# Moving the operand splits in front of the attention units to other buffers, other engines and a later place

## The chip, the cores and the metric

The kernel runs on one core of one Trainium2 chip. A core has a matrix engine (TensorE, PE in the profile), three engines for elementwise work (VectorE or DVE, ScalarE or ACT, GpSimd or POOL), and queues that start DMAs (SP's, ACT's and POOL's). The metric is the device time of one execution in microseconds (us), lower is better. The kernel before was timed three times: 1029.26, 1029.71 and 1030.7 us, median 1029.71 us. One further execution was profiled.

## The reference: what is computed

One layer of a transformer-like block on 1024 latent tokens (a 16 by 64 grid) and 256 context tokens of width 1024. The part around the change is the two-dimensional neighbourhood attention: each token attends to an 8 by 16 window of the grid, with a learned relative position bias, and to all context tokens in the same softmax.

```python
u_x, q_x, k_x, v_x = _project(h_x, w_in[l])
u_c, q_c, k_c, v_c = _project(h_c, w_in[l])
...
s_loc = jnp.einsum('bnqhd,brnkhd->bhnqrk', q_r, k_b).astype(jnp.float32) * scale
s_loc = jnp.where(col_mask, s_loc + bias.astype(jnp.float32), -jnp.inf)
s_ctx = jnp.einsum('bnqhd,bkhd->bhnqk', q_r, k_ctx).astype(jnp.float32) * scale
s = jnp.concatenate([s_loc.reshape(B, H, NA_NCB, NA_QB, n_loc), s_ctx], axis=-1)
p = jax.nn.softmax(s, axis=-1).astype(v.dtype)
...
o = (jnp.einsum('bhnqrk,brnkhd->bnqhd', p_loc, v_b) + jnp.einsum('bhnqk,bkhd->bnqhd', p_ctx, v_ctx))
...
mix_x = jnp.concatenate([_pool_mixer(u_x, pool_w[l], pool_scale[l]), attn_x], axis=-1) @ w_out[l]
x = x + gt1 * _rmsnorm(mix_x, g_post_mix[l])
y_x = _sq_relu_mlp(_modulate(x, g_pre_mlp[l], sh2, sc2), w_mlp_in[l], w_mlp_out[l])
x = x + gt2 * _rmsnorm(y_x, g_post_mlp[l])
```

All numbers are float32.

## The kernel before, in words

**Products in parts.** To keep float32 accuracy, an operand of a product is split into a high part (rounded to the matrix engine's fp32r type) and a low part (what is left), and a product is three matmuls: high by high, high by low, low by high (function three, L197 to L200). A split is one copy for the high part and one subtraction for the low part: split (L156) makes the copy on ACT (L146) and the subtraction on DVE (L152).

**Keys and queries.** The eight heads are worked in four pairs j = 0 to 3. Keys and queries come from a seven-product scheme (Strassen's kind) with products called P1 to P7. Each product is made for K and for Q and for j = 0 and 1, and is twelve matmuls (half_product, L950); kept_product (L931) adds its bank into the tiles kT[j] and q. The list of steps in front of the attention, L959, ends with step 20 and 21 (P7 of K, j = 0 and 1) and step 22 and 23 (P4 of K, "the last key product"). P7 and P4 of Q (last_query, L1195) stand behind that loop. In the profile the K products write the banks pK, the last Q products the banks pqv.

**Parts of keys and queries.** key_parts(j, b) (L904) splits half b (columns 512 b to 512 b + 511) of kT[j] into kP{j}h and kP{j}l, and query_parts(j, b) (L910) splits q of pair j, half b, into qP{j}_{b}. Both go through apart (L894): with pool set, both instructions are POOL's (L896 and L897), otherwise ACT's and DVE's. Their buffers come from one of two sets: with spare set from the "hl" set of eight tiles (whl), which the weights of the seven products use as well, two for each; otherwise from the "pg" set of 33 tiles (page), which holds nearly everything else: tokens' parts (hx, S3h), kT, q, the bias tables, values and so on.

**Units.** The attention is 32 units i = 8 j + m: pair j, block m of 128 tokens. Around the first units the program's order is: scores(i) (PE, banks S; then two DVE instructions, L1033, one for each head e, which add the bias table and find the least value), the jobs of unit i (L1211), turn(i - 2) (18 or 22 transposes on PE, L1064, of which the first take shares[i - 2], a POOL copy rb, L1050), exps(i, 0), the kept turns (L1083, one on ACT and one on DVE), exps(i, 1) (ACT, L1044), last_query("P4", i) for i = 0 and 1, and values(i - 3) (PE, L1098). share(i - 1) is called inside scores(i), behind its first L1033: a reciprocal on DVE and the copy rb on POOL. The banks S of a unit are two, for e = 0 and 1, and there are two in all, so scores(i + 1) need the L1033 of unit i.

**The order.** A list scheduler places instructions and grants buffers; a set of in_order blocks fixes the program's order of each engine inside a block. The loop of steps is one block (pooling, L956), and what follows is another (projected, L1193), with POOL in a block of its own (first_pool, L1190). Between the two blocks the order on an engine is the scheduler's. On POOL, the program's order around the first units is: the tables' memsets (L872), two accumulating DMAs add_to(s3, s1a) at i = 1 and two at i = 2 (issued at L188, y<-y in the profile), rb at scores(i), and three table instructions (L885) for each call of built.

Of the kernel before, what the change touches and what calls it, by code (L numbers as in the profile page):

```python
# [11 lines left out]
F32 = mybir.dt.float32  # L12
# [68 lines left out]
def hybrid_block(ctx, tc, x, ctx_in, w_mod, b_mod, gp1, gp2, w_in, pool_w, rpb, w_out, w1, w2, vectors,  # L81
                 mask, edge, out):
    nc = tc.nc
    sub, mul, add = ALU.subtract, ALU.mult, ALU.add
# [59 lines left out]
    def high_part(src, hi, factor=1.0):  # L144
        if factor == 1.0:
            nc.scalar.copy(hi, src)  # L146
        else:
            nc.scalar.activation(hi, src, AF.Copy, scale=factor)
# [7 lines left out]
    def split(src, hi, lo, factor=1.0):  # L156
        high_part(src, hi, factor)
        low_part(src, hi, lo, factor)
# [112 lines left out]
    with tc.tile_pool(name="ps1", bufs=6, space=PSUM) as ps1, tc.tile_pool(name="tmp1", bufs=3) as tmp:  # L271
# [276 lines left out]
        for k in range(2):  # L548
            hi, lo = hx[0][k][:, :512], hx[0][k][:, 512:]
# [342 lines left out]
        kparts, qparts, kcs = [None] * 4, {}, []  # L892

        def apart(src, hi, lo, pool):  # L894
            if pool:
                nc.gpsimd.tensor_copy(hi, src)  # L896
                nc.gpsimd.tensor_tensor(lo, src, hi.bitcast(F32), sub)  # L897
            else:
                split(src, hi, lo)

        def part_page(name, spare):
            return whl.tile([P, 1024], F32R, tag="hl", name=name) if spare else page(name, F32R)

        def key_parts(j, b, spare=False, pool=False):  # L904
            if kparts[j] is None:
                kparts[j] = [part_page(f"kP{j}{n}", spare) for n in "hl"]
            bs = slice(b * 512, b * 512 + 512)
            apart(kT[j][:, bs], kparts[j][0][:, bs], kparts[j][1][:, bs], pool)

        def query_parts(j, b, spare=False, pool=False):  # L910
            t = part_page(f"qP{j}_{b}", spare)
            qparts[j, b] = t[:, :512], t[:, 512:]
            apart(qT[j][b], *qparts[j, b], pool)
# [42 lines left out]
        with in_order(ET.PE, ET.Pool, ET.Activation, ET.DVE, ET.SP) as pooling:  # L956
            banks = {of: [bank(f"p{of}{j}") for j in range(2)] for of in "KQ"}
            use(-1)
            for step, (n, of, j) in enumerate([(n, of, j) for n, of in products for j in range(2)]):  # L959
                half_product(n, of, j, banks[of])  # L960
                use(step)
                if step in (5, 9, 17):
                    name = {5: "S1", 9: "S4", 17: "S3"}[step]
                    parts = token_operand(name, sraw[name])
                if step in (5, 7, 9, 11, 17, 19):
                    next(parts)
                    next(parts)
                if step in (7, 11):
                    name = {7: "S4", 11: "S3"}[step]
                    sraw[name] = token_raw(name)  # L970
                if step == 14:
                    mask_page()
                if step == 20:
                    for _ in tables(0):
                        pass
                if step in (21, 22):
                    for g in range(2):
                        pool_mixed(2 * (step - 21) + g)
                kept_product(n, of, j, banks[of][j])
                if step == 10:  # L980
                    kcs += [page(f"kc{n}", F32R) for n in "hl"]
                    split(kcp, *kcs)
                if step == 20:
                    key_parts(0, 0)
                if step == 22:
                    query_parts(0, 0, True)


    with (
# [50 lines left out]
        def exps(i, e):  # L1040
            if e == 0:
                sums[i] = sm(f"su_{i}", 2, 4)
            sp = probs[i, e]
            nc.scalar.activation(sp, sp, AF.Exp, bias=least[i, e], scale=-1.0, accum_out=sums[i][:, e : e + 1])  # L1044
# [148 lines left out]
        with in_order(ET.PE, ET.Activation, ET.DVE, ET.SP) as projected:  # L1193

            def last_query(n, j):  # L1195
                half_product(n, "Q", j, last_queries)
                kept_product(n, "Q", j, last_queries[j])

            key_parts(0, 1)
            key_parts(1, 0, True)  # L1200
            query_parts(1, 0, True)
            last_query("P7", 0)
            key_parts(1, 1)
            last_query("P7", 1)
            key_parts(2, 0, True)
            query_parts(2, 0)

            table = [None] + [tables(j) for j in (1, 2, 3)]
            built = lambda j: next(table[j])
            out_of = lambda n: mod_out(n, accs[n])  # L1210
            jobs = {0: [(built, 1), (key_parts, 2, 1)], 1: [(built, 1)], 2: [(built, 1)], 3: [(built, 1)], 4: [(built, 1)],  # L1211
                    5: [(out_of, "a")], 6: [(out_of, "sc")], 7: [(query_parts, 1, 1, True, True)],
                    8: [(mixed_split, 0, True)], 9: [(built, 2), (out_of, "sh")],
                    10: [(columns_of, "sc", scale2), (built, 2)], 12: [(columns_of, "sh", s2), (built, 2)],
                    13: [(built, 2), (built, 2)], 14: [(query_parts, 3, 0, False, True)],
# [5 lines left out]
            for i in range(N + 4):  # L1221
                if i in LOADS:
                    weight_load(0, kks[LOADS.index(i)])
                if i == N:
                    t1 = [out_load(f"to1_{kk}w", kk, 1) for kk in (0, 1)]
                    b22 = [out_load(f"bo22_{kk}w", kk, 1) for kk in (2, 3)]
                    t3 = [out_load(f"to3_{kk}w", kk, 1) for kk in (2, 3)]
                    for to, kk in zip(t1, (0, 1)):
                        add_to(halved(to), out_block(kk, 0))
                if i == N - 2:  # L1230
                    G1 = gate_page("a")
                if i > 3:
                    weighed(i - 4)
                    if i % 8 == 3:
                        j = i // 8 - 1
                        add_to(s1a[j], heads[j][:, 512:])
                        add_to(sa2[j], heads[j][:, 512:])

                rest_of_bank = lambda name: pz[:, 256:]
                if i == 0:  # L1240
                    gain = mod_gain(gp1, att.tile([P, 256], F32, tag="gp", name="gpa"), nc.sync)
                if i == 4:
                    mod_gate("a", accs["a"], gain, rest_of_bank)
                    accs["sh"] = page("accsh2")
                    nc.sync.dma_start(accs["sh"], kept_row)
                if i == 5:
                    column_sums("sc", accs["sc"], rest_of_bank)
                if i == 8:
                    column_sums("sh", accs["sh"], rest_of_bank)
                if i in (1, 2):  # L1250
                    with tc.issue_after(pooling[ET.Pool]):
                        for k in (2 * i - 2, 2 * i - 1):
                            add_to(s3[k], s1a[k])
                if i in (5, 6):
                    for k in (2 * i - 10, 2 * i - 9):
                        nc.sync.dma_start(sa2[k], s3[k])
                if 8 < i < N and i % 8 == 7:
                    j = i // 8 - 1
                    add_to(heads[j][:, :512], sa2[j])
                low()  # L1260
                if i == N:
                    mixed_split(3)
                for n, at in enumerate(HALVES):
                    if at == i:
                        weight_split(n)
                if i < N:
                    scores(i)
                    for f, *args in jobs.get(i, ()):
                        f(*args)
                else:  # L1270

                    t = i - N
                    if t == 0:
                        x, s1 = [], halves_of("so1_")
                    if t % 2 == 0:
                        xs = ps_s.tile([P, 1024], F32, tag="S", name=f"pox{t}")
                        x += [xs[:, :512], xs[:, 512:]]
                    out_sums(x[t], "A11", wo, t, True)
                    nc.scalar.copy(s1[t], x[t])
                if 1 < i <= N + 1:  # L1280
                    turn(i - 2)
                    fifth_kept(i - 2)
                if i < N:
                    exps(i, 0)
                if 1 < i <= N + 1:
                    turn_kept(i - 2, 0, nc.scalar.copy)
                if i < N:
                    exps(i, 1)
                if 1 < i <= N + 1:
                    turn_kept(i - 2, 1, nc.vector.tensor_copy)  # L1290
                if i < 2:
                    last_query("P4", i)
                if i == N:
                    share(i - 1)
                if 2 < i <= N + 2:
                    values(i - 3)
                if i == 1:
                    query_parts(0, 1)
                if i > N:
                    out_operand("S1", i - N - 1, s1a[i - N - 1])  # L1300
# [752 lines left out]
```

## Time and profile before

| | before |
|---|---|
| median of 3 runs | 1029.71 us |
| profiled execution | 1031.34 us |
| span of its core, first to last instruction | 1029.6 us |
| PE busy | 1014.6 us, 99% of the span |
| DVE busy | 747.1 us |
| ACT busy | 546.8 us |
| POOL busy | 142.6 us |
| mean granted PE clock | 0.996 |
| first scores (unit 0) start | 220.80 us |
| scores of unit 2 start | 231.05 us |

Times within the profile count from the span's start. A row of the timeline gives start, duration, engine, line, operation, output <- inputs, shape and count; in brackets stands how long the engine had been idle before it and which instruction ended that. A row of windows gives, for a stretch, the busy time of each engine with the number of its instructions, the granted PE clock (1.00 is full speed), the share of the DMA engines and the GB/s.

### The profile page before, as it was taken

To read this page: it belongs to the slowest core of one execution; us is meant where nothing else is said; L and a number is where in the kernel's file an instruction comes from. 1 tells how busy PE (TensorE), PEld (TensorE's weight loads), DVE (VectorE), ACT (ScalarE), POOL (GpSimd) and SP (SyncE) were. 2 spreads that over 40 slices of the span, in tenths; PEclk is the share of its full clock that TensorE was granted. 3 is DMA by queue.
4 is the path that set the end of the run, shared out by engine and by line. 5 is a ranking of instruction groups with operands and counts; after the bars stand their busy time and mean duration, and the time that the engine had idled before them with its cause. 6 is when DMAs were issued, how large, how long until landed. Compare 5 with 4: busy or idle time off the path is not lost.

```text
span 1029.6 us, 16022 instructions
## 1 busy us (share of the span) xinstructions
PE 1014.6 (99%) x5910; PEld 840.7 (82%) x5910; DVE 747.1 (73%) x1160; ACT 546.8 (53%) x945; POOL 142.6 (14%) x225
## 2 busy tenths in 40 slices
PE   8999999999999999999999999999999999999997
PEld 7788888878898788888888888888888888888885
DVE  5588757857886687878998888755766666556576
ACT  7573254338897556776655554545543334334431
POOL 3011110126774311410000000000000000000001
PEclk9999999999999999999999999999999999999999
DMA  9999798623338966785776667537967766556556
GB/s 343 333 255 338 248 257 303 204 48 97 74 94 215 214 180 190 262 229 186 260 262 202 216 204 230 189 123 242 337 218 263 254 222 220 201 183 190 172 185 210
DMA packets 123134, 222.70 MB, mean 216 GB/s; under 512 B 9456, under 2 KB 55152, under 8 KB 123056
## 3 DMA queue, kind: packets, MB, share of 16 engines
q1 hardware_dynamic: 96560, 171.14, 50.6%
q0 software_dynamic: 9360, 19.58, 9.4%
q10 hardware_dynamic: 17136, 30.97, 8.1%
q8 instruction: 46, 0.75, 0.3%
q14 instruction: 32, 0.26, 0.1%
HBM read 168.16 MB, written 52.45 MB: 214 GB/s over the span
## 4 chain that ended last, share of the span: by engine, by line
PE 94%; DMA 2%; DVE 1%; issue 0%; ACT 0%; POOL 0%; SPq 0%; DVEq 0%; POOLq 0%; ACTq 0%
PE pu L449 4%; PE pa L1098 4%; PE S L1018 3%; PE phz L198 3%; PE phv L198 3%; PE phx L198 3%; PE pyx L198 3%; PE phx L200 3%; PE pyx L200 3%; PE phz L200 3%; PE pyx L199 3%; PE pyv L198 3%; PE pyz L199 3%; PE pyv L199 3%; PE phv L200 3%; PE pyz L198 3%
## 5 line engine op out<-in xcount | busy, mean ns | idle before, releaser
L1044 ACT ACTIVATE sp<-sp,nm 128x640 f32<-128x640 f32 (+1 forms) x64 | 51.5, 804 | 11.4 <-DVE nm L1033 5.3
L1033 DVE CUSTOM_DVE_ANT_0 sp<-S,tab 128x640 f32<-128x640 f32 (+1 forms) x56 | 44.5, 795 | 14.2 <-PE pz L1064 10.3
L1639 ACT ACTIVATE c<-c 128x512 f32<-128x512 f32 x48 | 30.3, 631 | 44.8 <-DVE c L1759 25.7
L146 ACT CAST wpS<-S 128x512 fp32r<-128x512 f32 x64 | 38.8, 616 | 27.4 <-PE phv L200 9.5
L198 PE MATMUL phx<-thB,wpA 128*128 128x512 f32 x128 | 50.2, 392 | 0.0
L200 PE MATMUL phx<-thB,wpA 128*128 128x512 f32 x128 | 49.8, 389 | 0.0
L199 PE MATMUL phx<-tlB,wpA 128*128 128x512 f32 x128 | 49.8, 389 | 0.0
L152 DVE TENSOR_TENSOR wpS<-S,wpS 128x512 fp32r<-128x512 f32 x64 | 43.4, 685 | 7.4 <-ACT wpS L146 7.4
L140 POOL TENSOR_TENSOR ry<-vy,nhalf 128x1 f32<-128x1 f32 x8 | 5.9, 740 | 281.5 <-DVE vy L138 281.5
L1640 ACT ACTIVATE c<-c 128x512 f32<-128x512 f32 x48 | 30.3, 630 | 15.6 <-DVE sa L1722 12.1
L198 PEld LDWEIGHTS phx<-thB,wpA 128*128 128x128 f32 x128 | 24.0, 188 | 5.4 <-ACT s L1690 0.5
L200 PEld LDWEIGHTS phx<-thB,wpA 128*128 128x128 f32 x128 | 24.0, 188 | 5.1
L199 PEld LDWEIGHTS phx<-tlB,wpA 128*128 128x128 f32 x128 | 24.0, 188 | 4.8
L1098 PE MATMUL pa<-pt,v 128*64 128x128 f32 x352 | 25.9, 280 | 0.2
L1083 DVE COPY pt<-T 128x512 f32<-128x512 f32 x32 | 21.9, 686 | 5.6 <-PE T L1064 5.6
L198 PE MATMUL phz<-thB,wpS 128*128 128x512 f32 x64 | 25.0, 391 | 0.0
L198 PE MATMUL phv<-thT,wpA 128*128 128x512 f32 x64 | 25.0, 391 | 0.0
L199 PE MATMUL phz<-tlB,wpS 128*128 128x512 f32 x64 | 24.9, 390 | 0.0
L199 PE MATMUL phv<-tlT,wpA 128*128 128x512 f32 x64 | 24.9, 389 | 0.0
L200 PE MATMUL phz<-thB,wpS 128*128 128x512 f32 x64 | 24.9, 389 | 0.0
L199 PE MATMUL phy<-tlT,wpS 128*128 128x512 f32 x64 | 24.9, 389 | 0.0
L200 PE MATMUL phy<-thT,wpS 128*128 128x512 f32 x64 | 24.9, 389 | 0.0
(1133 smaller groups left out, 3431.8 us busy)
## 6 DMA issues: line engine op xcount, KB each, us to landing
b<-in_w SPq DMA_DIRECT2D x64, 512.0 KB, 4.6
hrS<-hdS SPq DMA_DIRECT2D x32, 512.0 KB, 5.0
hrA<-hdA SPq DMA_DIRECT2D x24, 512.0 KB, 5.8
wm<-in_w_mod SPq DMA_DIRECT2D x16, 512.0 KB, 9.8
wa_0w<-in_w SPq DMA_DIRECT2D x16, 512.0 KB, 5.0
wa_1w<-in_w SPq DMA_DIRECT2D x16, 512.0 KB, 4.4
hdA<-c ACTq DMA_DIRECT2D x32, 256.0 KB, 2.9
hdS<-sa ACTq DMA_DIRECT2D x32, 256.0 KB, 3.2
```

The lines of the kernel that those rows point to most:

```text
L146: nc.scalar.copy(hi, src)
L152: nc.vector.tensor_tensor(lo, src, hi.bitcast(F32), sub)
L198: nc.tensor.matmul(ps, ahi, bhi, start=first, stop=False, skip_group_check=more)
L199: nc.tensor.matmul(ps, ahi, blo, start=False, stop=False, skip_group_check=more)
L200: nc.tensor.matmul(ps, alo, bhi, start=False, stop=last, skip_group_check=more)
L449: nc.tensor.matmul(pus[b][j], wk(wgt, k, low, j * P, P), r, start=(k == 0 and n == 0), stop=(k == KT - 1 and n == 2))
L1018: nc.tensor.matmul(S[e][:, c0 : c0 + k[0].shape[1]], q[n_q][hs, cols], k[n_k][hs], start=(n_q + n_k == 0), stop=(n_q == 1))
L1033: nc.vector.tensor_tensor_reduce(out=to, in0=s, in1=bt, scale=1.0, scalar=BIG, op0=add, op1=ALU.min, accum_out=nm)
L1044: nc.scalar.activation(sp, sp, AF.Exp, bias=least[i, e], scale=-1.0, accum_out=sums[i][:, e : e + 1])
L1098: nc.tensor.matmul(pa[e * HD : (e + 1) * HD, cols], v[:, f : f + HD], turns[i][:, e, c] if c < 4 else fifths[i][:, :, (e + 1) * HD : (e + ...
L1639: nc.scalar.activation(r, src, AF.Relu)
L1640: nc.scalar.activation(r, r, AF.Square)
```

## The change

The first keys' parts, key_parts(0, 0), were split at step 20 into page buffers; now they are split at step 22, behind that step's kept_product, into spare buffers of the "hl" set. query_parts(0, 0) leaves step 22 and stands first behind the loop. Of the second pair, the query part (1, 0) is now made by POOL, and the two key parts leave the stretch around last_query("P7", ...) for the jobs of unit 0, into page buffers where they had spare ones. Of the third pair, both key parts and query part (2, 0) are made at the end of unit 0, behind exps(0, 1), with the high part on ACT and the low part on POOL (the new value "lo" of pool).

```diff
         def apart(src, hi, lo, pool):
-            if pool:
-                nc.gpsimd.tensor_copy(hi, src)
-                nc.gpsimd.tensor_tensor(lo, src, hi.bitcast(F32), sub)
-            else:
+            if not pool:
                 split(src, hi, lo)
+                return
+            (nc.scalar.copy if pool == "lo" else nc.gpsimd.tensor_copy)(hi, src)
+            nc.gpsimd.tensor_tensor(lo, src, hi.bitcast(F32), sub)
...
-                if step == 20:
-                    key_parts(0, 0)
                 if step == 22:
-                    query_parts(0, 0, True)
+                    key_parts(0, 0, True)
...
+            query_parts(0, 0, True)
             key_parts(0, 1)
-            key_parts(1, 0, True)
-            query_parts(1, 0, True)
+            query_parts(1, 0, True, True)
             last_query("P7", 0)
-            key_parts(1, 1)
             last_query("P7", 1)
-            key_parts(2, 0, True)
-            query_parts(2, 0)
...
-            jobs = {0: [(built, 1), (key_parts, 2, 1)], 1: [(built, 1)], 2: [(built, 1)], 3: [(built, 1)], 4: [(built, 1)],
-                    5: [(out_of, "a")], 6: [(out_of, "sc")], 7: [(query_parts, 1, 1, True, True)],
+            jobs = {0: [(built, 1), (key_parts, 1, 0), (key_parts, 1, 1)], 1: [(built, 1)], 2: [(built, 1)], 3: [(built, 1)],
+                    4: [(built, 1)], 5: [(out_of, "a")], 6: [(out_of, "sc")], 7: [(query_parts, 1, 1, True, True)],
...
                 if i < N:
                     exps(i, 1)
+                if i == 0:
+                    key_parts(2, 0, True, "lo")
+                    key_parts(2, 1, True, "lo")
+                    query_parts(2, 0, False, "lo")
```

## The prediction

> **What bounds the kernel now.** I read the page first: its busy times and its chain that ended last.
>
> ```profile
> span 1029.6 us, 16022 instructions
> PE 1014.6 (99%) x5910; PEld 840.7 (82%) x5910; DVE 747.1 (73%) x1160; ACT 546.8 (53%) x945; POOL 142.6 (14%) x225
> PE 94%; DMA 2%; DVE 1%; issue 0%; ACT 0%; POOL 0%; SPq 0%; DVEq 0%; POOLq 0%; ACTq 0%
> ```
>
> PE is the bound, and the chain is PE's for 94%. So the change can only be worth what PE loses near the first units. The view of windows shows that loss, first in two stretches of 3 us, then in three of 3.41 us.
>
> ```profile
> 216.00:219.00 3.00, 2.40 (x11) 1.76 (x10) 3.00 (x6) 0.32 (x1) 2.05 (x3) 1.00 0.34 59
> 219.00:222.00 3.00, 1.91 (x17) 1.22 (x15) 2.91 (x6) 2.65 (x6) 0.00 (x0) 1.00 0.84 145
> ...
> 219.28:222.69 3.41, 1.81 (x16) 1.18 (x15) 3.36 (x6) 3.06 (x7) 0.00 (x0) 1.00 0.85 147
> 222.69:226.10 3.41, 3.41 (x9) 2.62 (x9) 3.41 (x9) 0.78 (x2) 0.00 (x0) 0.50 0.26 92
> 232.90:236.30 3.40, 2.69 (x42) 2.37 (x44) 2.86 (x10) 2.92 (x8) 1.61 (x5) 1.00 1.09 248
> ```
>
> From 216 to 222 PE is busy for 4.31 of 6 us while DVE is hardly free (5.91), and from 222.69 to 226.10 PE's granted clock is 0.50: nine matmuls where there is room for about fifteen. The timeline of DVE says why DVE is late.
>
> ```profile
> 205.45 0.69 DVE L946 TENSOR_TENSOR kT<-kT,pK 128x512 f32<-128x512 f32 x1 [0.32 <-PE pK L200]
> 214.35 0.69 DVE L152 TENSOR_TENSOR kP0l<-kT,kP0h 128x512 fp32r<-128x512 f32 x1 [8.21 <-PE pqv L200]
> 216.16 0.68 DVE L946 TENSOR_TENSOR kT<-kT,pK 128x512 f32<-128x512 f32 x1
> 219.96 0.69 DVE L948 TENSOR_TENSOR kT<-pK,kT 128x512 f32<-128x512 f32 x1
> 224.78 0.68 DVE L1033 CUSTOM_DVE_ANT_1 sp<-S,tab 128x512 f32<-128x512 f32 x1
> ```
>
> DVE stands 8.21 us before kP0l, step 20's low part, and a PE matmul of the last Q products releases it. That matmul makes nothing that kP0l reads; it reads S3h, tokens' parts in page buffers. So kP0l waits for a page. Counting tiles in the code gives the same: at step 20 I find 32 of 33 pages live (values 5, y 4, tables 2, mask 1, kT 4, q 4, context keys 2, sums 2, S3h 4, hx 4), so kP0h finds one and kP0l none. Behind it on DVE stand the additions that free pK's banks and everything that the first units need, up to L1033 at 224.78. PE's timeline shows what that costs.
>
> ```profile
> 207.97 0.39 PE L198 MATMUL pK<-hx,wKT4h 128*128 128x512 f32 x1
> 210.69 0.39 PE L198 MATMUL pqv<-S3h,wQT3h 128*128 128x512 f32 x1
> 216.90 0.50 PE L198 MATMUL pK<-hx,wKT4h 128*128 128x512 f32 x1 [0.60 <-DVE kT L946]
> 220.80 0.39 PE L1018 MATMUL S<-kch,qP 64*128 64x256 f32 x2 [0.88 <-DVE kT L948]
> 221.47 0.31 PE L1018 MATMUL S<-kP0h,qP 64*128 64x256 f32 x2
> 222.51 0.63 PE L198 MATMUL pqv<-hx,wQT4h 128*128 128x512 f32 x1 [0.72 <-DVE q L946]
> 227.05 0.44 PE L1018 MATMUL S<-kP0h,qP 64*128 64x384 f32 x2
> 228.12 0.50 PE L198 MATMUL pqv<-hx,wQT4h 128*128 128x512 f32 x1
> 231.05 0.44 PE L1018 MATMUL S<-kP0h,qP 64*128 64x384 f32 x2
> 232.05 0.21 PE L1064 MATMUL pa<-ident,rb 64*128 64x64 f32 x1
> 234.05 0.44 PE L1018 MATMUL S<-kP0h,qP 64*128 64x384 f32 x1 [0.36 <-DVE nm L1033]
> 234.86 0.21 PE L1064 MATMUL pa<-ident,rb 64*128 64x64 f32 x1
> ```
>
> P4 of K for j = 1 has no bank at 210.69, so both P7 products of Q run ahead of it; it starts at 216.90 behind a gap of 0.60, scores of unit 0 follow a gap of 0.88, P4 of Q one of 0.72 and at the half clock.
>
> **The change, part by part.** *Step 20.* kP0l's wait goes: its new buffers are those of P7's key weights, read last by the product that ends at 207.97. What is late next on DVE: additions to kT, each behind its PE product. P4 of K, j = 1, then finds its bank (the addition of P7's second bank, due at 208.2) and PE runs P4, P7 and P7 without a gap. A product takes 210.69 - 207.97 = 2.72, so the three end at 210.69 + 3 x 2.72 = 218.85, and unit 0's scores start there and not at 220.80. Their query part and key parts, four instructions on ACT and DVE at 0.6 to 0.7 each, fall between 211 and 217; moved to the front of the block they are hidden by the two P7 products (5.44 us). Should the small buffers come late, with P4's key weights at 213.4, nothing is lost: kP0l now stands behind the addition that frees P4's bank, and the P7 products cover it.
>
> *Up to unit 2.* Scores of unit 0 take about 0.75 (220.80 to 221.47 and a last pair), the first P4 of Q 2.82 (twelve at 2.72 / 12, and 0.1 for the first), scores of unit 1 1.07 (227.05 to 228.12) and 0.1 to change over, the second P4 2.93 (228.12 to 231.05). Unit 2's scores start at 218.85 + 0.75 + 2.82 + 0.1 + 1.07 + 2.93 = 226.5, against 231.05: 4.5 us won. DVE can follow: five splits stood before L1033 of unit 0, none does now; two come behind it.
>
> *Second pair.* Its key parts now want two pages. By the count, kP0's two pages aren't taken, kT0 and the first q page come free before 216, S3h's four by 219; tables, U and kP1 want five: free at no cost. If the count is off, ACT waits in kP1h as DVE did in kP0l, and the exps queue behind it (second rival). Its query part costs POOL a cast and a subtraction, 2 us between 213.5 and 215.5, in front of memsets that nothing waits for.
>
> *Third pair: POOL's queue.* This is what I charge. ACT makes kP2's high parts behind exps(0, 1), and POOL its low parts in front of i = 1's two accumulating DMAs and rb of unit 0. Rows of ACT (a high part, the first exp, the end of the second), of POOL, and a PE row that waits for it:
>
> ```profile
> 219.20 0.62 ACT L146 CAST kP1h<-kT 128x512 fp32r<-128x512 f32 x1
> 225.50 0.72 ACT L1044 ACTIVATE sp<-sp,nm 128x512 f32<-128x512 f32 x1 [2.63 <-DVE nm L1033]
> 226.83 0.18 ACT L1044 ACTIVATION_READ_ACCUMULATOR sp<-sp,nm 128x1 f32 x1
> 229.45 1.27 POOL L885 TENSOR_TENSOR tab<-msk,U 128x128 f32<-128x128 f32 x3
> 230.67 1.75 POOL L188 DMA_DIRECT2D y<-y  x2
> 250.00 1.28 POOL L897 TENSOR_TENSOR qP<-q,qP 128x512 fp32r<-128x512 f32 x1
> 261.25 0.91 POOL L188 DMA_DIRECT2D y<-f  x1
> 262.43 0.92 POOL L1050 COPY rb<-ri 128x128 f32<-128x128 f32 x1
> 263.41 0.27 PE L1064 MATMUL pa<-ident,rb 64*128 64x64 f32 x1 [0.34 <-POOL rb L1050]
> ```
>
> L1033 of unit 0 moves from 224.78 to 219.85 (behind its scores), so the first exp from 225.50 to 220.57. The second ends 227.01 - 225.50 = 1.51 later, at 222.1, and kP2's first high part at 222.7. POOL makes three low parts at 1.25 (a little under the 1.28 of the row, since starts overlap), to 226.5; two DMAs and rb take 262.43 + 0.92 - 261.25 = 2.1, so rb is there at 228.6. PE wants it 1.0 behind the start of unit 2's scores (231.05 to 232.05), at 227.5: it waits 1.1. POOL goes on with three table instructions (1.22 from 229.45 to 230.67) and two DMAs and rb of unit 1 (2.1): 228.5 + 1.22 + 2.1 = 231.8, and turn(1) starts at 231.85. Undisturbed it would start 3.81 behind unit 2's scores (231.05 to 234.86, the gap of 0.36 in it), at 230.3. So POOL gives back 1.5 of the 4.5 us: turn(1) starts at 231.85 against 234.86, and **3.0 us stay won**. From then on rb is in time: that of unit 2 needs 1.22 and 0.3 more on POOL, to 233.4, and PE reaches it behind turn(1), values and scores of unit 4, past 235. Of the later units nothing changes but two pages held to unit 15 (I count 31 in use there). The row at 263.41 shows that rb behind two DMAs does hold PE.
>
> *Sum.* The profiled execution took 1031.34 us, 1.63 above the median. 1031.34 - 3.0 = 1028.3; against the median, 1029.71 - 3.0 = **1026.7 us**, 0.29% faster. Bounds: with no POOL wait, 4.5, 1025.2; with the half clock again, below.
>
> [...] A POOL instruction can be stretched by DVE:
>
> ```profile
> 204.01 1.43 POOL L885 TENSOR_TENSOR tab<-msk,U0w 128x128 f32<-128x128 f32 x1
> 203.60 1.53 DVE L154 SCALAR_TENSOR_TENSOR wQT4l<-wQT4w,wQT4h 128x1024 fp32r<-128x1024 f32 x1 [0.18 <-ACT wQT4h L148]
> L154 DVE SCALAR_TENSOR_TENSOR wQT2l<-wQT2w,wQT2h x1: 1227/1227/1227, 161.6 to 161.6; 128x1024 fp32r<-128x1024 f32 x1
> L885 POOL TENSOR_TENSOR tab<-msk,U x36: 436/450/470, 229.5 to 293.3; 128x128 f32<-128x128 f32 x36
> ```
>
> Beside a DVE instruction with two operands in SBUF a POOL instruction took 1.43 for 0.45, and DVE's 1.53 for 1.23. [...] By my times DVE's two kP1l end at 222.3 (219.85 and four instructions 0.6 apart), just ahead of POOL's first low part, and L1033 reads one operand from PSUM; a slip of 0.5 us makes one or two overlaps, 0.98 each.
>
> The half clock followed a stretch in which PE was busy 1.81 of 3.41 us, and did not follow one with 2.69 of 3.40. With waits of 1.1 and 1.5 and some 2 us of work between them, PE would be busy for 1.9 to 2.3 of some 3.41 us: between the two rows. [...]
>
> **The rivals.**
> 1. *The half clock comes back* behind POOL's waits. It costs up to 3.41 x 0.5 = 1.7 us where PE is the bound: 1026.7 + 1.7 = 1028.4 us, no measurable change. For it: the stretch above; against it: matmuls fill most of units 2 to 4.
> 2. *The page wait moves to kP1h* (slower). Place: ACT, in front of exps(0, 0). If no page is free, the next come from hx when the second P4 of Q has run its first terms, about 225.7 instead of 220.0. Then the exps, kP2h, POOL's queue, rb of units 0 and 1 all come 5.7 later: 1026.7 + 5.7 = 1032.4 us. It decides from 3.0 us of wait on, and is measurably slower from 5.1. For it: kP0l waited 8.21 on the same set; against it: my count.
> 3. *POOL's queue is no bound*: the DMAs are issued earlier or rb comes in time: 1025.2 us. For it: POOL is busy for no more than 14% of the span. Against it: the order on POOL is the program's.
> 4. *Contention on POOL*: one or two overlaps at 0.98, both on the way to rb: 1027.7 to 1028.7 us. For it: the rows above; against it: the 0.4 us between my two times.
>
> **How the numbers follow.** 0.2% is 2.06 us, about what a measurement of this kernel can tell from no change. Forecast 0.48 (faster); rival 3 0.15 (faster); rival 1 0.14 (same); rival 4 0.11 (0.03 faster, 0.08 same); rival 2 0.12 (slower). Faster 0.66, same 0.22, slower 0.12. The range goes from a little below rival 3, 1024.9, up over rivals 1 and 4 to 1029.5, for both at once; rival 2 lies outside.
>
> **What would show it.** kP0l without a wait of over 1 us; P4 of K in front of the last Q products; unit 0's scores near 218.9 and clock 1.00 from 216 to 227 (step 20 right). PE waiting for rb L1050 at unit 2 and 3, some 1.1 and 1.5 us (POOL's charge right); no such rows, and rival 3 holds. A wait on ACT at kP1h shows rival 2; a window of 0.50 clock after 228 rival 1; L897 over 2 us rival 4. My prediction is wrong if the units' pace later, above all in units 8 to 16 where two more pages are held, gets slower than before.

## The result, and the profile after

The changed kernel took 1028.16 us (median of its 16 runs; 15 lie at 1027.47 to 1029.14) against 1030.22 us (1029.26 to 1030.7) for the kernel before, run in turn with it: ratio 0.9982, 95% interval 0.9974 to 0.999, so 2.06 us or 0.2% faster. The sixteenth run, 5072.97 us, is a slow one whose cause is not known, and the ratio leaves it out. The forecast was 1026.7 us; its range, 1024.9 to 1029.5, holds the time. The profiled execution took 1028.11 us.

The page of after, its span, its busy times and its chain that ended last:

```profile
span 1026.3 us, 16024 instructions
PE 1012.1 (99%) x5910; PEld 839.0 (82%) x5910; DVE 746.8 (73%) x1156; ACT 546.0 (53%) x944; POOL 148.9 (15%) x230
PE 94%; DMA 2%; POOL 1%; ACT 1%; issue 1%; DVE 1%; SPq 0%; POOLq 0%; DVEq 0%; ACTq 0%
```

PE is still the bound. It does the same 5910 matmuls and is busy for 2.5 us less than in the profile of before (1014.6), and POOL for 6.3 us more. The windows of after, with the columns of those in the prediction:

```profile
216.00:219.00 3.00, 3.00 (x14) 2.25 (x12) 1.30 (x2) 1.14 (x2) 0.65 (x3) 1.00 0.22 54
219.00:222.00 3.00, 3.00 (x22) 2.45 (x22) 2.63 (x7) 1.21 (x3) 0.00 (x0) 1.00 0.38 119
228.00:231.00 3.00, 2.05 (x34) 1.65 (x30) 2.65 (x7) 1.91 (x6) 3.00 (x8) 1.00 1.03 211
231.00:234.00 3.00, 2.22 (x46) 1.78 (x47) 2.33 (x6) 2.07 (x7) 3.00 (x9) 1.00 1.01 216
```

The two stretches in which PE had stood for 1.69 of 6 us are full, and the granted clock is 1.00 in all four. The loss has moved: between 228 and 234 PE stands for 1.73 us, and POOL is busy for all of it. The timeline of after shows both, first PE:

```profile
210.80 0.39 PE L198 MATMUL pK<-hx,wKT4h 128*128 128x512 f32 x1
213.52 0.39 PE L198 MATMUL pqv<-S3h,wQT3h 128*128 128x512 f32 x1
219.05 0.39 PE L1016 MATMUL S<-kch,qP 64*128 64x256 f32 x2
226.99 0.44 PE L1016 MATMUL S<-kP0h,qP 64*128 64x384 f32 x2
228.78 0.27 PE L1062 MATMUL pa<-ident,rb 64*128 64x64 f32 x1 [0.63 <-POOL rb L1048]
230.10 0.44 PE L1016 MATMUL S<-kP0h,qP 64*128 64x384 f32 x1 [0.32 <-DVE nm L1031]
232.02 0.27 PE L1062 MATMUL pa<-ident,rb 64*128 64x64 f32 x1 [0.78 <-POOL rb L1048]
234.44 0.44 PE L1016 MATMUL S<-kP0h,qP 64*128 64x384 f32 x2
```

(The first line is P4 of K, j = 1, now ahead of P7 of Q, the second. The third is unit 0's scores, the fourth unit 2's, the last unit 4's. Of after, L1016, L1031, L1046, L1048, L1062 and L1081 are L1018, L1033, L1048, L1050, L1064 and L1083 of before, and L898 and L899 make the high and low part on one given engine each.) POOL, in the same profile:

```profile
214.44 1.71 POOL L899 TENSOR_TENSOR qP<-q,qP 128x512 fp32r<-128x512 f32 x1
222.90 2.56 POOL L899 TENSOR_TENSOR kP2l<-kT,kP2h 128x512 fp32r<-128x512 f32 x2 [6.25 <-ACT kP2h L898]
225.41 1.30 POOL L899 TENSOR_TENSOR qP<-q,qP 128x512 fp32r<-128x512 f32 x1
226.65 1.78 POOL L188 DMA_DIRECT2D y<-y  x2
227.83 0.90 POOL L1048 COPY rb<-ri 128x128 f32<-128x128 f32 x1
228.61 1.32 POOL L885 TENSOR_TENSOR tab<-msk,U 128x128 f32<-128x128 f32 x3
229.83 1.84 POOL L188 DMA_DIRECT2D y<-y  x2
```

From 222.9 on POOL never rests: three low parts, two DMAs, rb, three table instructions, two more DMAs, rb. Each of the two PE waits ends when one of the copies rb does. On DVE the wait for a page is gone: kP0l stands right behind the addition to kT. On ACT a shorter one is there in its place: kP1h stands 2.48 us for a matmul of the last Q products, which makes nothing that kP1h reads. The first exp, the third row, does not wait for it but for DVE's least values:

```profile
211.82 0.68 DVE L152 TENSOR_TENSOR kP0l<-kT,kP0h 128x512 fp32r<-128x512 f32 x1
217.12 1.14 ACT L146 CAST kP1h<-kT 128x512 fp32r<-128x512 f32 x2 [2.48 <-PE pqv L200]
220.79 0.72 ACT L1042 ACTIVATE sp<-sp,nm 128x512 f32<-128x512 f32 x1 [2.53 <-DVE nm L1031]
```

### The profile page after: what moved, and what is told of

Read it like the earlier page. It is cut to its first block, busy times and chain, and to the rows that moved or that the text cites. A ratio compares the mean times of both kernels' runs of the same rounds, so it can differ in the third digit from the quotient of the medians.

```text
span 1026.3 us, 16024 instructions
## 1 busy us (share of the span) xinstructions
PE 1012.1 (99%) x5910; PEld 839.0 (82%) x5910; DVE 746.8 (73%) x1156; ACT 546.0 (53%) x944; POOL 148.9 (15%) x230
## 4 chain that ended last, share of the span: by engine, by line
PE 94%; DMA 2%; POOL 1%; ACT 1%; issue 1%; DVE 1%; SPq 0%; POOLq 0%; DVEq 0%; ACTq 0%
PE pu L449 4%; PE pa L1096 4%; PE phz L198 3%; PE phv L198 3%; PE pyx L198 3%; PE phx L198 3%; PE phx L200 3%; PE pyv L200 3%; PE pyx L200 3%; PE pyz L200 3%; PE pyv L199 3%; PE phz L199 3%; PE pyz L199 3%; PE phv L199 3%; PE phx L199 3%; PE phz L200 3%
## 5 line engine op out<-in xcount | busy, mean ns | idle before, releaser
L1031 DVE CUSTOM_DVE_ANT_0 sp<-S,tab 128x640 f32<-128x640 f32 (+1 forms) x56 | 44.5, 794 | 14.1 <-PE pz L1062 10.3
L1081 DVE COPY pt<-T 128x512 f32<-128x512 f32 x32 | 21.9, 686 | 5.8 <-PE T L1062 5.8
L198 PE MATMUL phv<-thT,wpA 128*128 128x512 f32 x64 | 25.0, 391 | 0.0
L200 PE MATMUL phz<-thT,wpS 128*128 128x512 f32 x64 | 24.9, 389 | 0.0
L200 PE MATMUL phv<-thT,wpA 128*128 128x512 f32 x64 | 24.9, 389 | 0.0
```

Of the source, the lines that this page charges most:

```text
L198: nc.tensor.matmul(ps, ahi, bhi, start=first, stop=False, skip_group_check=more)
L200: nc.tensor.matmul(ps, alo, bhi, start=False, stop=last, skip_group_check=more)
L1031: nc.vector.tensor_tensor_reduce(out=to, in0=s, in1=bt, scale=1.0, scalar=BIG, op0=add, op1=ALU.min, accum_out=nm)
L1081: copy(turns[i].rearrange("p e i t -> p (e i) t")[:, :, h * HD : (h + 1) * HD], turned[i][h].rearrange("p (a t) -> p a t", a=8))
```

## The experiments

Every run was timed in turn with the kernel before on the same chip; the ratio is to those runs, with its 95% interval, and is what kernels are compared by (the medians of before itself were 1029.6 to 1030.2 us from one series to the next). All positions are read from the PE timeline of each profile; the first product of P4 of K (at 207.97 in before) shows how far the earlier part of an execution had shifted.

| kernel | median us | ratio (interval) | P4 of K | unit 2's scores | unit 4's scores | first out product |
|---|---|---|---|---|---|---|
| before, first profile | 1029.71 | | 207.97 | 231.05 | 237.41 | 320.78 |
| before, second profile | 1030.19 | 1.0 (0.9991 to 1.0009) | 208.00 | 230.24 | 236.59 | 319.87 |
| after, first profile | 1028.16 | 0.9982 (0.9974 to 0.999) | 208.08 | 226.99 | 234.44 | 317.74 |
| after, second profile | 1027.96 | 0.998 (0.9971 to 0.999) | 208.09 | 226.97 | 234.45 | 317.73 |
| first pair alone | 1026.35 | 0.9962 (0.995 to 0.9974) | 207.88 | 226.79 | 233.13 | 316.43 |
| first pair undone | 1032.24 | 1.0023 (1.0014 to 1.0032) | 208.18 | 228.98 | 236.38 | 321.99 |
| place alone | 1028.35 | 0.9982 (0.9973 to 0.9991) | 208.20 | 228.62 | 234.98 | 318.26 |
| buffers alone | 1027.02 | 0.9967 (0.9955 to 0.998) | 209.24 | 228.29 | 234.64 | 317.91 |
| first and second pair | 1026.51 | 0.9964 (0.995 to 0.9978) | 208.05 | 226.97 | 233.36 | 316.64 |
| DMAs ahead | 1027.22 | 0.9966 (0.9954 to 0.9978) | 207.96 | 226.87 | 233.56 | 316.83 |
| low parts on DVE | 1029.13 | 0.9984 (0.9976 to 0.9993) | 208.14 | 227.05 | 235.58 | 318.91 |
| query part on POOL | 1026.78 | 0.9969 (0.9958 to 0.9981) | 207.97 | 226.89 | 233.12 | 316.44 |
| gap filled | 1029.41 | 0.9994 (0.9985 to 1.0002) | 208.03 | 230.27 | 236.62 | 319.90 |

**First pair alone: which part gains.** Into the kernel before went the first pair's change and nothing else; since the second pair's first keys then find no small buffers, they go to pages.

```diff
-                if step == 20:
-                    key_parts(0, 0)
                 if step == 22:
-                    query_parts(0, 0, True)
+                    key_parts(0, 0, True)
...
+            query_parts(0, 0, True)
             key_parts(0, 1)
-            key_parts(1, 0, True)
+            key_parts(1, 0)
```

> The first pair's part alone: key_parts(0, 0) behind step 22 in small buffers, query_parts(0, 0) first behind the loop; the second pair's key parts stay where they were but take pages, since the small set has no room for them; the third pair's parts stay where they were, on ACT and DVE. Theory (the page wait of kP0l is what cost PE its gaps and its clock): P4 of K stands ahead of the last Q products, unit 0's scores start near 218.9, no rb wait at units 2 and 3; DVE has five splits in front of L1033 of unit 0 again, which may hold unit 1's scores by up to 1 us: 1026.5 to 1028.3 us. Rival (the gain comes from clearing the splits of pairs two and three out of DVE's way): no more than 0.5 us below the kernel before, 1029.7 us or more.

It is faster than both kernels. No PE wait for rb is left; what PE waits for before unit 3's scores is DVE, 0.48 and 0.37 us:

```profile
228.98 0.44 PE L1016 MATMUL S<-kP0h,qP 64*128 64x384 f32 x1 [0.48 <-DVE nm L1031]
229.79 0.44 PE L1016 MATMUL S<-kP0h,qP 64*128 64x384 f32 x1 [0.37 <-DVE nm L1031]
```

So the first pair carries the whole gain, and the rest of the change takes part of it back.

**First pair undone.** The other way round: after, with the first keys' parts back at step 20 in pages.

```diff
+                if step == 20:
+                    key_parts(0, 0)
                 if step == 22:
-                    key_parts(0, 0, True)
+                    query_parts(0, 0, True)
...
-            query_parts(0, 0, True)
```

> The changed kernel with the first pair's part undone: key_parts(0, 0) at step 20 in pages, query_parts(0, 0) at step 22; all else as changed. Theory: kP0l waits about 8 us for a page as before, the last Q products run ahead of P4 of K, unit 0's scores start at 220 or later, 1029 to 1030.5 us. Rival (splits of pairs two and three in DVE's way): about 1028.2 us as the changed kernel.

The wait of 8.21 us before kP0l is back to the hundredth (DVE timeline), and with it two of the three gaps of PE, 0.60 and 0.88 us:

```profile
214.55 0.69 DVE L152 TENSOR_TENSOR kP0l<-kT,kP0h 128x512 fp32r<-128x512 f32 x1 [8.21 <-PE pqv L200]
```

But it is slower than before, which neither theory had. Its unit 4 still starts 0.2 us earlier than in the second profile of before; most of the time goes at unit 8, where a copy on ACT and one on DVE, both into new tiles pt, stand still, and PE behind them (ACT's row, then PE's):

```profile
247.72 0.58 ACT L1083 COPY pt<-T 128x512 f32<-128x512 f32 x1 [1.68 <-DMA ga<-acca]
248.78 0.24 PE L1064 MATMUL pa<-ident,rb 64*128 64x64 f32 x1 [1.73 <-DVE f L1108]
```

In this kernel the first and the second pair's key parts hold four pages together, two more than in before or after, and pt would then wait for one as kP0l does. That is argued from the count of buffers; the row alone shows only that a copy waits for a DMA whose data it doesn't read.

**Place or buffers.** The first pair's edit has two parts, tried one by one. Place alone moves the key parts to step 22 and leaves them in pages; buffers alone leaves them at step 20 and puts them in small buffers.

```diff
-                if step == 20:
-                    key_parts(0, 0)
                 if step == 22:
-                    query_parts(0, 0, True)
+                    key_parts(0, 0)
...
+            query_parts(0, 0, True)
```

> Before, with the first keys' parts at step 22 instead of 20, still in page buffers, and their query part first behind the loop: the place without the buffers. Second and third pair as before. Theory (a page was wanted): kP0l waits still, until S3h or other pages come free, but P4 of K no longer stands behind it: PE runs P4 of K in front of the last Q products as in the run with the first pair's parts moved and in small buffers (1026.35 us), without the gaps at 217 and 220; scores of unit 0 wait for kP0l and start between 219 and 220.5; 1026.5 to 1028.5 us. Rival (the buffers carry the gain): the wait moves to kP0h or kP0l with the Q products' additions queued behind it on DVE, PE loses as much as before, unit 0's scores at 220.8 or later: 1029.7 us or more.

```diff
                 if step == 20:
-                    key_parts(0, 0)
+                    key_parts(0, 0, True)
...
-            key_parts(1, 0, True)
+            key_parts(1, 0)
```

> Before, with the first keys' parts left at step 20 but in small buffers, and the second pair's first half in pages in exchange: the buffers without the place. The small buffers come free when P7's key weights have been read, at 207.97. Theory (the wait for a page was the loss, the place is worth little): DVE waits about 2 us (205.9 to 208.3) instead of 8.21, P4 of K starts some two matmuls late but has no gap of over 0.5 us; unit 0's scores at 219 to 219.3, clock 1.00: 1026.3 to 1027.2 us. Rival (the place matters too): DVE is late by these 2 us through the first units, unit 2's scores come at 228 or later: 1028 us or more.

DVE's timeline with place alone, and then with buffers alone:

```profile
217.24 0.69 DVE L152 TENSOR_TENSOR kP0l<-kT,kP0h 128x512 fp32r<-128x512 f32 x1 [4.24 <-PE pqv L200]
```

```profile
209.87 0.69 DVE L152 TENSOR_TENSOR kP0l<-kT,kP0h 128x512 fp32r<-128x512 f32 x1 [2.46 <-ACT kP0h L146]
```

At the later place in pages kP0l still waits 4.24 us, for a matmul of a P7 product of Q, as before; in small buffers at the old place it waits 2.46 us, behind kP0h, which waits on ACT for the K product that ends at 209. So the set of buffers is what it waits for. The place helps in another way: with place alone P4 of K no longer stands behind kP0l and runs ahead of the last Q products, and of PE's three gaps one is left, 0.84 us at 220.98. Measured from P4 of K, the first out product comes after 111.87 us in the second profile of before, 110.06 with place alone, 108.67 with buffers alone and 108.55 with both (319.87 - 208.00, and so on): place alone is worth 1.8, buffers alone 3.2, both 3.3 us. The absolute time of buffers alone has 1.2 us in it that its profile lost before P4 of K, where the change is not: PE stands 1.60 us at 24.49 for an operand that ACT makes, where it stands 0.43 in the second profile of before.

**The second and third pair.** To the first pair alone was added the second pair as in after; what is missing to after is the third pair on POOL.

```diff
-            key_parts(1, 0)
-            query_parts(1, 0, True)
+            query_parts(1, 0, True, True)
             last_query("P7", 0)
-            key_parts(1, 1)
...
-            jobs = {0: [(built, 1), (key_parts, 2, 1)], 1: [(built, 1)], 2: [(built, 1)], 3: [(built, 1)], 4: [(built, 1)],
+            jobs = {0: [(built, 1), (key_parts, 1, 0), (key_parts, 1, 1), (key_parts, 2, 1)], 1: [(built, 1)], 2: [(built, 1)], 3: [(built, 1)], 4: [(built, 1)],
```

> The run with the first pair's parts alone (1026.35 us) with the change's second pair added: its query part on POOL between the last Q products, its key parts in unit 0's jobs. The third pair stays on ACT and DVE where it was before. It differs from the kernel after in the third pair alone. Theory: the third pair's low parts on POOL, in front of rb, are the whole loss against 1026.35, and the second pair's move costs nothing: 1026.0 to 1026.7 us, no PE wait for rb at units 2 and 3, unit 4's scores at 233.1 to 233.3. Rival: the second pair's move costs a part (two low parts between the least values of units 0 and 1 on DVE, or the query part on POOL): 1027 us or more, unit 2's scores later than 227.0 or waits of PE for DVE's nm of over 1 us.

The time stays that of the first pair alone, and PE's row of turn(1) has no wait:

```profile
230.84 0.21 PE L1062 MATMUL pa<-ident,rb 64*128 64x64 f32 x1
```

In after that row stands at 232.02. So the second pair's move is free, and the third pair's low parts on POOL are the loss: 1.15 us at turn(1) (0.03 of the 1.18 is the shift at P4 of K), 1.1 us at unit 4's scores and at the first out product.

**What in POOL's queue holds rb.** In after, once the four accumulating DMAs were issued ahead of unit 0's scores, and once the third pair's low parts went to DVE.

```diff
-                if i in (1, 2):
+                if i == 0:
                     with tc.issue_after(pooling[ET.Pool]):
-                        for k in (2 * i - 2, 2 * i - 1):
+                        for k in range(4):
```

> The changed kernel with the four accumulating DMAs of i = 1 and 2 issued at i = 0, in front of unit 0's scores, where POOL has nothing to do for 6 us. Theory (rb of units 0 and 1 is late because POOL's queue holds it): no PE wait for rb at units 2 and 3, unit 1's turn some 1.4 us earlier, 1026.8 us. Rival (another wait, DVE's least values or the exps, is right behind rb): gain under 0.5 us, 1027.7 us or more.

```diff
                 if i == 0:
-                    key_parts(2, 0, True, "lo")
-                    key_parts(2, 1, True, "lo")
-                    query_parts(2, 0, False, "lo")
+                    key_parts(2, 0, True)
+                    key_parts(2, 1, True)
+                    query_parts(2, 0)
```

> The changed kernel with the third pair's three low parts on DVE and not on POOL, at the same place. Theory: rb of unit 0 comes 3.7 us earlier on POOL and holds nothing; DVE has 1.8 us more in front of the addition that follows the first P4 of Q, which it has room for: 1026.8 us. Rival (DVE's room is needed): L1033 of unit 1 comes 1 us or more late and PE waits for it, 1027.7 us or more.

With the DMAs ahead, no wait for rb is left, but unit 4's scores come 0.9 us earlier than in after (0.8 counted from P4 of K) and not 1.4 (PE timeline):

```profile
229.40 0.44 PE L1016 MATMUL S<-kP0h,qP 64*128 64x384 f32 x1 [0.82 <-DVE nm L1031]
```

Behind rb stand DVE's least values, and they hold PE from 228 on even with rb in time. With the low parts on DVE it is worse: 1.19 us of wait for them, and the clock falls behind it (PE's row, then two windows of the same kernel):

```profile
229.95 0.43 PE L1016 MATMUL S<-kP0h,qP 64*128 64x384 f32 x1 [1.19 <-DVE nm L1031]
```

```profile
228.00:231.00 3.00, 1.44 (x25) 1.05 (x23) 2.54 (x7) 1.71 (x6) 2.47 (x5) 1.00 0.99 303
231.00:234.00 3.00, 3.00 (x43) 2.88 (x43) 2.48 (x7) 2.93 (x8) 1.66 (x6) 0.63 0.71 120
```

Most of its 11 runs lie in two groups, four at 1027.5 to 1027.8 with a mean granted clock of 0.998, and five at 1029.1 to 1029.3 with 0.996 or 0.997; the profiled run, 1029.19, is of the second.

**One split more off DVE.** To the first pair alone: the query part (0, 1), whose low part stands on DVE just ahead of unit 2's least values, goes to POOL behind rb.

```diff
-            jobs = {0: [(built, 1), (key_parts, 2, 1)], 1: [(built, 1)], 2: [(built, 1)], 3: [(built, 1)], 4: [(built, 1)],
+            jobs = {0: [(built, 1), (key_parts, 2, 1)], 1: [(built, 1)], 2: [(query_parts, 0, 1, False, True), (built, 1)], 3: [(built, 1)], 4: [(built, 1)],
...
-                if i == 1:
-                    query_parts(0, 1)
```

> The run with the first pair's parts alone (1026.35 us), with one split more taken from DVE: the query part (0, 1), whose low part stands on DVE in front of unit 2's least values, goes to POOL behind unit 1's rb. Theory: those least values start 0.6 us earlier, so PE's waits for them in front of unit 3's scores (0.48 and 0.37 us) shrink to 0.4 us or less in sum; POOL has the part ready at about 231.4, before unit 4's scores want it at 232.6, and rb of unit 2 still comes by 233.0: 1025.7 to 1026.1 us. Rival: POOL is late again, as in the kernel after: PE waits for rb of unit 2 or for the query part in front of unit 4's scores, and the time is 1026.4 us or more.

It gains nothing. The first of the two waits falls from 0.48 to 0.37 us, and DVE's row says why (DVE timeline):

```profile
228.08 0.82 DVE L1031 CUSTOM_DVE_ANT_0 sp<-S,tab 128x640 f32<-128x640 f32 x1 [0.40 <-PE pz L1062]
```

DVE now waits for PE, where in the first pair alone the same instruction starts at 228.10 without a wait. (The row names a later matmul; the last of unit 2's scores ends at 228.05.) Unit 2's least values can't begin before its scores are there, and unit 3's scores need the banks: what is left, 0.37 us in front of each of unit 3's two banks, is the hand-over between the two engines. POOL is not late, as the rival had it: PE has no wait for rb.

**Is the profile of before a usual execution?** Three more runs: before again, before with its gap filled by six transposes that serve nothing, and after again.

> The kernel before, unchanged, for a second profile of it. Its profiled execution had a stretch at a granted clock of 0.50 (222.69 to 226.10 us), took 1031.34 us and stands above the median of the same kernel's runs, 1030.1 us. Theory A: the half clock is in some executions only, so that the median stands between two groups of runs. Then runs fall into two groups some 1.2 to 1.7 us apart (3.41 us at half the clock cost up to 1.7), and a second profile may show clock 1.00 throughout and unit 2's scores at about 229.5 to 230. Rival: the half clock is in every execution; then a second profile shows 0.50 again behind unit 0's scores and unit 2's scores at 231.0, and the runs are one group.

```diff
+                    if i == 0:
+                        for _ in range(6):
+                            nc.tensor.transpose(pz[:, 256:384], ident, ident)
```

> Before, with six transposes of a constant into an unused bank (they serve nothing else) behind unit 0's scores, where PE is idle for 0.72 us; nothing waits for them and no other engine's order changes. Theory: it was the idle time of PE (1.81 busy of 3.41 us) that halved the clock. With more busy time it stays at 1.00, the first P4 product of Q runs at full speed, and unit 1's scores no longer wait for it but for L1033 of unit 0, which ends at about 226.0: they start at 226.1 instead of 227.05, so unit 2's scores come about 0.9 earlier, at 230.1: 0.9 us faster than the kernel before where that has the half clock. Rival: six short transposes don't count enough, or the clock goes by what came before 219: again 0.50 behind 222 and a time within 0.3 us of the kernel before.

> The kernel after, unchanged, for a second profile. Theory: its waits of 0.6 and 0.8 us for rb at units 2 and 3 and the start of unit 4's scores 2.2 us earlier than in the undisturbed profile of before (236.59) come again, so unit 4's scores at 234.3 to 234.6; and its one wait of 0.32 us at 351.57 us, where the second set of out products waits for a small DVE result (ns), is another thing that comes in some executions only. If the half clock can follow the rb waits in some executions, as three of its 15 runs at 1028.8 to 1029.1 us suggest, some of these runs are again some 0.9 us above the others. Rival: the wait at ns belongs to the change, and comes again with 0.3 us or more.

The second profile of before took 1029.54 us against 1031.34 of the first. Its PE timeline has the same gaps, 0.60, 0.88 and 0.73 us, and its windows the same lack of work, but no half clock:

```profile
216.93 0.50 PE L198 MATMUL pK<-hx,wKT4h 128*128 128x512 f32 x1 [0.60 <-DVE kT L946]
220.86 0.39 PE L1018 MATMUL S<-kch,qP 64*128 64x256 f32 x2 [0.88 <-DVE kT L948]
222.56 0.50 PE L198 MATMUL pqv<-hx,wQT4h 128*128 128x512 f32 x1 [0.73 <-DVE q L946]
230.24 0.44 PE L1018 MATMUL S<-kP0h,qP 64*128 64x384 f32 x2
```

```profile
219.00:222.00 3.00, 1.96 (x17) 1.27 (x15) 2.91 (x6) 2.63 (x6) 0.00 (x0) 1.00 0.83 142
222.00:225.00 3.00, 2.44 (x11) 2.02 (x12) 3.00 (x6) 0.93 (x2) 0.00 (x0) 1.00 0.52 144
```

So the half clock is in some executions of before only. It cost 0.8 us at unit 4's scores and 0.9 at the first out product (320.78 - 319.87), not 1.7: in the undisturbed profile PE waits for DVE's least values instead (the first P4 of Q starts its last matmul at 225.19 and not at 226.72, but unit 1's second bank waits until 226.19, where the first profile starts both at 227.05). Most of the other 0.9 of the 1.8 us between the two executions arises at 354, at a second set of out products, the lines of the first profile of before, then of the first of after:

```profile
354.84 0.47 PE L198 MATMUL poz<-to_0h,S 128*128 128x512 f32 x1 [0.53 <-DVE ns L1455]
```

```profile
351.57 0.47 PE L198 MATMUL poz<-to_0h,S 128*128 128x512 f32 x1 [0.32 <-DVE ns L1454]
```

The second profile of each kernel doesn't have this wait. On DVE, ns stands behind an instruction that waits for a DMA (first profile of after, then second):

```profile
350.74 0.69 DVE L1165 TENSOR_TENSOR mp<-pox,Ga 128x512 f32<-128x512 f32 x1 [2.62 <-DMA to_3w<-to_1w]
```

```profile
349.99 0.69 DVE L1165 TENSOR_TENSOR mp<-pox,Ga 128x512 f32<-128x512 f32 x1 [2.49 <-DMA to_3w<-to_1w]
```

The row starts 0.75 us later in the one than in the other. The delay is older than the DMA that the row names: POOL's f<-ss, which waits for the DMA ss<-f, starts 0.74 us later too (POOL timeline, first profile of after, then second):

```profile
344.67 0.86 POOL L188 DMA_DIRECT2D f<-ss  x1 [4.00 <-DMA ss<-f]
```

```profile
343.93 0.86 POOL L188 DMA_DIRECT2D f<-ss  x1 [3.29 <-DMA ss<-f]
```

Yet POOL issued ss<-f at 333.90 in the one and at 333.91 in the other. From that issue to the row that waits for it is 10.77 and 10.02 us in the two profiles of after, and 10.98 and 10.04 in the two of before. So a DMA that took longer delays ns, in both kernels, and the two executions of after, equal to 0.01 us at 317.7, end 0.7 us apart (spans 1026.3 and 1025.6). The rival, that the wait at ns comes with the change, fell.

The theory that the half clock is in some executions only held, at a price of 0.9 us and not of 1.2 to 1.7. The mean granted clock that is listed with each run says the same: 3.41 us at the half clock take 0.0017 off it, and of the 64 runs of before that were timed with these experiments 22 have 0.997 or less and a median of 1030.6 us, 42 have 0.998 or more and a median of 1029.7.

Filling the gap left the time the same: the profile shows clock 1.00 and unit 2's scores at 230.27, as the second profile of before. Nine of its 11 runs lie at 1029.2 to 1029.5, where 17 of 38 runs of before lie at 1029.2 to 1029.6 and the rest at 1029.8 to 1031.4; of its other two, 1029.98 and 1031.42, the second has a mean clock of 0.947, and why is not known. That fits a half clock that comes less often, but so few runs don't show it.

## Why the prediction came out as it did

The direction and the mechanism held, and so did the sum as long as it is set against the profiled execution: 1028.3 us against 1028.11. Against the median it was 1.5 us too fast (1026.7 for 1028.16): 0.5 of it is the base, 1029.71 in three runs and 1030.22 in the 16 that were timed with after, and 0.9 the gain, 2.06 for 3.0. That the sum met the profiled execution so closely is in part luck: unit 2 came 0.5 us later than forecast, POOL's charge was 0.35 smaller, and the late DMA was in both profiled executions. By its own steps:

- **Step 20: right.** kP0l waits no more; P4 of K stands before the last Q products, PE has no gap from 206 to 228. Unit 0's scores start at 219.05, forecast 218.85, with 0.11 of the difference in the later start of P4 of K. That the wait was for a page, and not for anything kP0l reads, was an inference from a count of tiles; the runs with place and buffers apart bear it out.
- **Up to unit 2: nearly right.** 226.99 for 226.5; 0.11 is again the start, most of the rest lies in unit 0 and the first P4 of Q (3.89 us to unit 1's scores, 3.67 forecast).
- **Second pair: right in its cost, wrong in that nothing waits.** The page came free at 217.12, with the P7 product that reads S3h, and ACT stood 2.48 us for it. That is rival 2's place and its sign, "A wait on ACT at kP1h shows rival 2", but short of the 3.0 us from which it decides: the exps did not wait for ACT, so rival 2's time is out. The units' later pace, named as the sign of being wrong, is unchanged: from unit 4's scores to the first out product it is 83.28 us in the second profile of before, and the same in that of after.
- **POOL's queue: right in place and time, too dear in its cost.** rb of unit 0 was forecast for 228.6, and PE takes it at 228.78; turn(1) was forecast for 231.85, and came at 232.02. The two waits, forecast at 1.1 and 1.5 us, are 0.63 and 0.78, with 0.32 for DVE's least values between them. POOL kept its times, but PE came to them later: "Undisturbed it would start 3.81 behind unit 2's scores … at 230.3" was right in the distance, 3.87 us with the third pair off POOL, and too early by the 0.5 us that unit 2's scores were late, so that turn(1) starts at 230.84 there. So POOL's charge is 1.15 and not 1.5 us. Rival 3, that the queue is no bound, is out: the two waits are there, and taking away POOL's work in two ways took them away.
- **Contention (rival 4): there, but beside the path.** The two parts kP2l, on the way to rb, took 1.28 us each. The query part on POOL took 1.71 us, where the one at 225.41 took 1.30, beside a DVE split (214.93 to 216.71, 1.78 us for the 0.68 of the split in front of it), and no PE wait follows. L1033, which reads one operand from PSUM, shows no such effect in before: the three L885 from 260.03, beside two L1033 from 260.18 to 261.81, took 1.27 us together, and none of its 36 took over 0.47. What makes the longer rows longer no trace shows.
- **The half clock (rival 1): not in either profile of after**, although PE was busy for only 2.05 and 2.22 of 3 us in two stretches in a row. None of the few runs of after at 1028.8 to 1029.1 was profiled, but their mean granted clock is 0.998, as in the others, which speaks against it there too.
- **The step that failed: "against the median, 1029.71 - 3.0".** The 3.0 us was read from one profiled execution that I knew to be 1.63 us above the median, and 0.8 of it was the half clock, which that execution had and the second profile of the same kernel had not. Between the undisturbed profiles unit 4's scores moved by 2.2 us (236.59 - 234.45, and 0.09 for the later P4 of K), and these executions took 1029.54 and 1027.36: 2.2 us. That is what the change is worth where nothing else happens, and the medians show 2.06. Had I asked where the 1.63 us above the median lay, the window at clock 0.50, priced at up to 1.7, was the candidate in plain sight.

So what the change wins is 3.3 us in the first pair, and what it gives back is 1.1 on POOL. The version with the first pair alone is 0.38% faster than before, about twice the gain of the full change (0.18%).

## What to carry to other kernels

When an engine waits on a matmul or a DMA whose data the waiting instruction does not touch, count the tiles of its buffer set: the cure is another set, and the place matters less (3.2 and 1.8 us here). Before a saving read from one profile is taken off a median, ask what that execution has in it that others lack; a stretch at a lower clock is the first thing to look at, and a second profile of the same kernel can settle it for the price of one run. Work that leaves a loaded engine lands in another one's queue: list what stands behind it there, and try each part of a bundled change alone, since one may pay for another.

## What the runs showed of the hardware

The half clock came and went with the same gaps. In before, gaps of 0.60, 0.88 and 0.72 us and 1.91 of 3 us busy were followed by 3.41 us at 0.50 in one profile; gaps of 0.60, 0.88 and 0.73 us and 1.96 of 3 us were followed by full clock in the other. The kernel with the low parts on DVE, with 1.44 of 3 us busy, had a mean clock of 0.63 in the 3 us that followed; after, with 2.05 and 2.22 of 3 us busy in two stretches in a row, stayed at 1.00. What decides between the two the traces do not show.

In these profiles a POOL row that is queued behind others counts the time from before its predecessor's end. The copy rb is listed with 0.90 us behind two DMAs that end at 228.43 and itself ends at 228.73, 0.30 later; in the kernel with the first and second pair, where nothing stands in front of it, the same copy takes 0.29:

```profile
229.29 0.29 POOL L1048 COPY rb<-ri 128x128 f32<-128x128 f32 x1 [0.54 <-DVE ri L1046]
```

One accumulating DMA, ss<-f, took 0.75 us longer in one execution of after than in another (10.77 and 10.02 us from its issue to the row that waits for it); what made it longer was not traced. Together with the half clock, 0.9 us at the first out product, this sets the spread that a change of 0.2% has to be read against here.
